# Selecting experts for one half of the tokens beside the gates of the other half

## The chip, the core and the metric

The kernel runs on one NeuronCore of a Trainium2 chip. TensorE multiplies (PE in the profile; its weight loads are PEld), VectorE (DVE), ScalarE (ACT) and GpSimd (POOL) work element by element, and SyncE (SP) issues the DMA transfers. The metric is the device time of one execution in microseconds, and lower is better; times of a kernel are given as the median of the runs shown.

## The reference, cut to what matters

The program is a network of two blocks for 256 tokens with 1024 features, all in fp32. The first block (feed-forward layers, a state-space mixer, neighbourhood attention) and the attention part of the second are not touched. The last stage, `peer`, is:

```python
q = (ht @ w_q).reshape(T, HEADS, 2, half)              # 8 heads, 2 halves of 128 features
s = einsum('thcd,hcnd->thcn', q, sub_keys)             # scores against 128 keys for each half
s1, i1 = top_k(s[:, :, 0], 16)
s2, i2 = top_k(s[:, :, 1], 16)
cand_s = s1[..., :, None] + s2[..., None, :]           # 16 x 16 candidates for a head
top_s, pos = top_k(cand_s, 16)                         # the best 16; pos gives the pair (i1, i2)
gates = softmax(top_s)
experts = i1 * 128 + i2
out = x + sum over (head, k) of gates * gelu(h . u[expert]) * v[expert]
```

## The kernel before

Matmuls are in fp32r with each operand split into a high and a low part, and three products (high by high, high by low, low by high). All weights of the program are one long row of 741 chunks of 128x1024, numbered in the order of use: 469 to 484 are the queries' weights (`peer_q`, one chunk for each of 16 blocks of queries), 485 to 612 the experts' first table (`ut`, two chunks for each of 64 tiles) and 613 to 740 the second table (`v`). The class `Weights` loads a chunk (`w`, 4 buffers), casts its high part on ScalarE (`whi`, line 92) and subtracts the low part (`wlo`), both with 3 buffers. The subtraction is on VectorE (line 96), or on GpSimd (line 94) where the chunk's number modulo 8 is in `ws.on_pool`.

The stage does not gather experts. It computes all of them densely: 64 tiles `c` of the first product (lines 246 to 248), each followed by a GELU into `st` and a store to DRAM (`sd`); then the second product (line 1241), for which each tile is fetched again and multiplied by the gates `gt` (`gate(n)`, line 1221, and a split into high and low parts). The tiles 62 and 63 come first in the second product, since they need no fetch. `gt` has a gate for each of 128 x 128 experts and each of 256 tokens, and fills the large tile `gbig`, in which the scratch of the selection also lies.

The gates come from two generators. `topk_gen(tt)` selects for the 128 tokens of half `tt`: 12 pairs of calls of `top16`, each with ten steps on VectorE (MAX, MAX_INDEX, MATCH_REPLACE), then six 2048-wide steps. `g_gen` takes four tokens at a time: one-hot rows `hot_a` and `hot_g` on VectorE (lines 1131 and 1132), four small matmuls that multiply them (line 1140), and a copy into `gt` on ScalarE (line 1143).

The order is that of the program as the scheduler of the recording layer places it on each engine; within an engine instructions run in that order. The class `Sched` decides what is written between the matmuls: generators in `sc.bg` run one after another, each step yields its cost, and each `tick(budget)` lets so much cost through. Before, `topk_gen(0)`, `topk_gen(1)` and `g_gen()` are appended behind the last query.

`qevac(c)` (line 1163) scales the queries of block `c` from PSUM on VectorE, and `scores(c)` (line 1041 on TensorE, line 1044 on ScalarE) multiplies them by the keys. `by_token` (line 1155) transposes `h`, which `hr` holds after a trip through DRAM. `norm.split` makes the low parts of the first product's input (line 352).

Of the kernel before, what the change touches and what calls it, by code (L numbers as in the profile page):

```python
# [22 lines left out]
T = 256  # L23
# [146 lines left out]
def tile_kernel(ctx: ExitStack, tc: tile.TileContext, A: dict, start: int = 0, end: int = 10):  # L170
# [6 lines left out]
    small = ctx.enter_context(tc.tile_pool(name="small", bufs=3))  # L177
# [840 lines left out]
    def peer(norm):  # L1018
        with tc.tile_pool(name="peer", bufs=2) as p:
            gbig = p.tile([128, 32768], F32, name="gbig", bufs=1)  # L1020
            gt = gbig.rearrange("p (i t) -> p i t", t=T)
            off = [0]

            def carve(n, dt=F32):
                a = gbig[:, off[0]:off[0] + n]
                off[0] += n
# [4 lines left out]
            hr = carve(8 * T).rearrange("p (c t) -> p c t", t=T)  # L1031
            nc.sync.dma_start(hr, hd)
            nc.sync.dma_start(keys, A["keysT"])
            scr = [carve(16 * 128).rearrange("p (c n) -> p c n", n=128) for _ in range(2)]
            i1T, i2T, gaT = (carve(T) for _ in range(3))
# [10 lines left out]
            def top16(rows):  # L1046

                for v, ix, src, tmp in rows:
                    V.max(v[:, 0:8], src)
                for v, ix, src, tmp in rows:  # L1050
                    V.max_index(ix[:, 0:8], v[:, 0:8], src)  # L1051
                for v, ix, src, tmp in rows:
                    V.match_replace(tmp, v[:, 0:8], src, -3.0e38)  # L1053
                for v, ix, src, tmp in rows:
                    V.max(v[:, 8:16], tmp)
                for v, ix, src, tmp in rows:
                    V.max_index(ix[:, 8:16], v[:, 8:16], tmp)  # L1057

            def topk_gen(tt):
                val = carve(256).rearrange("p (c k) -> p c k", k=16)  # L1060
# [17 lines left out]
                yield 1.5  # L1078
                for c in range(0, 8, 2):
                    top16([(tv[:, c + i], pos[:, c + i], cand[:, c + i], tmp[i]) for i in range(2)])  # L1080
                    yield 2.2
# [3 lines left out]
                V.tensor_tensor(e, tv, tv[:, :, 0:1].to_broadcast([128, 8, 16]), op=ALU.subtract)  # L1085
# [15 lines left out]
                yield 1.5  # L1101
# [3 lines left out]
                for c, rank in ((0, af), (1, bf)):  # L1105
                    r = carve(128)
                    V.tensor_tensor(oh.rearrange("p (k a) -> p k a", a=16), rank[:, :, None].to_broadcast([128, 128, 16]),
                                    iota[:, None, 0:16].to_broadcast([128, 128, 16]), op=ALU.is_equal)
                    yield 2.2
                    o4 = oh.rearrange("p (h k a) -> p h k a", h=8, a=16)  # L1110
                    V.tensor_tensor(o4, o4, ix2[:, :, c][:, :, None, :].to_broadcast([128, 8, 16, 16]), op=ALU.mult)
                    yield 2.2
                    V.tensor_reduce(r, oh.rearrange("p (k a) -> p k a", a=16), AX.X, ALU.add)
                    yield 2.2
                    res.append(r)
# [3 lines left out]
                for n, dst in enumerate((i1T, i2T, gaT)):  # L1119
                    S.copy(dst[:, tt * 128:(tt + 1) * 128], pt[:, n * 128:(n + 1) * 128])  # L1120
                yield 0.2

            def g_gen():


                def hots(t0):
                    a = p.tile([128, 4, 128], F32, name="hot_a")
                    g = p.tile([128, 4, 128], F32, name="hot_g")
                    for i in range(4):
                        t = slice(t0 + i, t0 + i + 1)  # L1130
                        V.tensor_scalar(a[:, i], iota, i1T[:, t], None, op0=ALU.is_equal)  # L1131
                        V.tensor_scalar(g[:, i], iota, i2T[:, t], gaT[:, t], op0=ALU.is_equal, op1=ALU.mult)
                    return a, g
                nxt_ = hots(0)
                yield 1.3
                for t0 in range(0, T, 4):
# [4 lines left out]
                    if t0 + 4 < T:  # L1141
                        nxt_ = hots(t0 + 4)
                    S.copy(gt[:, :, t0:t0 + 4].rearrange("p i t -> p t i"), ps.rearrange("p (t i) -> p t i", t=4))
                    yield 1.5


            ht = carve(2 * D).rearrange("p (a d) -> p a d", a=2)
            htd = dram.tile([128, 2, D], F32, name="htd")

            def by_token():  # L1150
                for n in range(4):
                    tt, f = divmod(n, 2)
                    pt = aux()
                    for i in range(4):
                        PE.transpose(pt[:, i * 128:(i + 1) * 128], hr[:, f * 4 + i, tt * 128:(tt + 1) * 128], ident)
# [33 lines left out]
            sgs = {}  # L1189
            for c in range(64):  # L1190
                if c == topk_end:
                    ws.on_pool = ()
                ps = mmtile()
                for i in range(2):
# [4 lines left out]
                    sc.tick(2.35 if c < topk_end else 1.12)  # L1199
# [10 lines left out]
            cx = {}  # L1210
# [7 lines left out]
            def gate(n):  # L1218
                c = V_ORDER[n]
                sg = sgs.pop(c)  # L1220
                tc.keep_in_program_order(V.tensor_mul(sg, sg, gt[:, 2 * c:2 * c + 2, :]))
                i = (n % 4) * 2
                ch, cl = (x[:, i:i + 2] for x in norm.x[:2])
                split2(ch, cl, sg)
                cx[n] = (ch, cl)

            gate(0)
# [225 lines left out]
```

## Time and profile before

| | |
|---|---|
| median of 3 runs | 2394.49 us (2390.14 to 2395.95) |
| the profiled execution | 2397.36 us, span 2395.4 us |
| TensorE busy | 2330.9 us (97%) |
| VectorE busy | 1807.1 us (75%) |
| ScalarE busy | 1327.1 us (55%) |
| GpSimd busy | 373.0 us (16%) |
| mean granted clock of TensorE | 0.99 |

The span goes from the first to the last instruction of the profiled execution; the rest of its time lies around it. A busy share is a mean over all stages, and TensorE's matmuls overlap, so that a gap in TensorE's work is read from the idle time ahead of an instruction, not from the share. The granted clock is 1.00 at 2.4 GHz and 0.5 at 1.2 GHz.

### The profile page before, as it was taken

What the parts mean: (1) busy time and instruction counts of PE and PEld (TensorE: products, weight loads), DVE (VectorE), ACT (ScalarE), POOL (GpSimd) and SP (SyncE); (2) the same over time, 40 slices, a digit from 0 to 9 for tenths busy, and PEclk for the clock granted to TensorE, in tenths of its full rate; (3) what the DMA queues carried; (4) which work ended last, traced back from release to release, by engine and by line L of the source; (5) the groups of instructions that cost most, each with busy time, mean ns of one, the idle gap of its engine ahead of it and who ended that gap; (6) DMA issues with size and microseconds to landing.
All of it is one profiled execution on the core that took longest, in us unless ns stands there. A gap on an engine that the chain in (4) does not pass through costs nothing.

```text
span 2395.4 us, 41145 instructions
## 1 busy us (share of the span) xinstructions
PE 2330.9 (97%) x15646; PEld 2127.0 (89%) x15646; DVE 1807.1 (75%) x3550; ACT 1327.1 (55%) x2081; POOL 373.0 (16%) x309
## 2 busy tenths in 40 slices
PE   8998799999999999999999999998999999999999
PEld 7887798988888889888889999998999999888887
DVE  6777788878768877777768766799777776666666
ACT  6555677746546554566545445554455565444443
POOL 1004788850010000030001000113300000000000
PEclk9999899999999999999999999999999999999999
DMA  6664565546565656435565445655655555777775
GB/s 212 191 191 139 175 197 194 190 142 195 189 190 171 188 186 194 158 125 177 187 189 179 150 137 182 223 177 189 203 183 188 186 189 188 250 242 242 242 241 187
DMA packets 138629, 452.51 MB, mean 189 GB/s; under 512 B 15552, under 2 KB 19648, under 8 KB 137920
## 3 DMA queue, kind: packets, MB, share of 16 engines
q1 hardware_dynamic: 138432, 449.89, 59.1%
q8 instruction: 123, 2.02, 0.3%
q14 instruction: 74, 0.61, 0.1%
HBM read 430.33 MB, written 19.50 MB: 188 GB/s over the span
## 4 chain that ended last, share of the span: by engine, by line
PE 69%; DVE 7%; issue 2%; ACT 1%; DMA 0%; POOL 0%; DVEq 0%; ACTq 0%; POOLq 0%; SPq 0%
PE mm L254 15%; PE aux L1241 15%; PE mm L247 9%; PE mm L248 9%; PE mm L246 9%; PE mm L255 8%; PE aux L1140 2%; DVE wlo L96 2%; DVE x L352 1%; ACT whi L92 1%; PE aux L733 0%; DVE gbig L1051 0%; PE aux L800 0%; DVE gbig L1053 0%; DVE gbig L1057 0%
## 5 line engine op out<-in xcount | busy, mean ns | idle before, releaser
L92 ACT CAST whi<-w 128x1024 fp32r<-128x1024 f32 x740 | 775.5, 1049 | 872.9 <-issue 328.5
L96 DVE TENSOR_TENSOR wlo<-w,whi 128x1024 fp32r<-128x1024 f32 x678 | 845.9, 1248 | 361.8 <-ACT whi L92 359.1
L248 PE MATMUL mm<-x,wlo 128*128 128x256 f32 x2472 | 706.1, 286 | 26.7 <-DVE wlo L96 22.0
L246 PE MATMUL mm<-x,whi 128*128 128x256 f32 x2472 | 718.7, 291 | 3.0 <-ACT acc L552 1.1
L247 PE MATMUL mm<-x,whi 128*128 128x256 f32 x2472 | 705.7, 286 | 2.3 <-DVE x L352 2.2
L254 PE MATMUL mm<-x,whi 128*128 128x512 f32 x1408 | 501.6, 400 | 10.0 <-DVE x L352 10.0
L248 PEld LDWEIGHTS mm<-x,wlo 128*128 128x128 f32 x2472 | 479.1, 194 | 28.6 <-DVE wlo L96 23.4
L246 PEld LDWEIGHTS mm<-x,whi 128*128 128x128 f32 x2472 | 479.1, 194 | 14.6 <-issue 8.4
L247 PEld LDWEIGHTS mm<-x,whi 128*128 128x128 f32 x2472 | 479.4, 194 | 4.2 <-DVE x L352 3.5
L255 PE MATMUL mm<-x,wlo 128*128 128x256 f32 x1408 | 398.6, 283 | 2.1 <-DVE wlo L96 2.1
L254 PEld LDWEIGHTS mm<-x,whi 128*128 128x128 f32 x1408 | 267.6, 190 | 73.7 <-DVE x L352 12.0
L1241 PE MATMUL aux<-whi,x 128*128 128x512 f32 x1024 | 274.1, 390 | 2.0 <-ACT x L362 2.0
L255 PEld LDWEIGHTS mm<-x,wlo 128*128 128x128 f32 x1408 | 270.0, 192 | 3.0 <-DVE wlo L96 2.9
L299 POOL TENSOR_TENSOR sqa<-sqa,sq 128x256 f32<-128x256 f32 x99 | 94.1, 951 | 1141.7 <-ACT sq L298 1135.3
L254 PE MATMUL mm<-a,whi 128*128 128x512 f32 x704 | 246.6, 395 | 0.0
L1241 PEld LDWEIGHTS aux<-whi,x 128*128 128x128 f32 x1024 | 192.2, 188 | 42.0 <-ACT x L362 2.2
L255 PE MATMUL mm<-a,wlo 128*128 128x256 f32 x704 | 197.6, 281 | 0.0
L94 POOL TENSOR_TENSOR wlo<-w,whi 128x1024 fp32r<-128x1024 f32 x62 | 166.7, 2690 | 159.3 <-ACT whi L92 151.1
L254 PEld LDWEIGHTS mm<-a,whi 128*128 128x128 f32 x704 | 132.1, 188 | 30.8
L1241 PE MATMUL aux<-wlo,x 128*128 128x512 f32 x512 | 157.8, 389 | 0.0
L255 PEld LDWEIGHTS mm<-a,wlo 128*128 128x128 f32 x704 | 133.4, 189 | 0.0
L1131 DVE TENSOR_SCALAR hot_a<-cst,gbig 128x128 f32<-128x128 f32 x256 | 72.0, 281 | 63.7 <-PE aux L1140 63.7
(265 smaller groups left out, 2801.2 us busy)
## 6 DMA issues: line engine op xcount, KB each, us to landing
w<-in_gu SPq DMA_DIRECT2D x175, 512.0 KB, 4.1
w<-in_ut SPq DMA_DIRECT2D x128, 512.0 KB, 3.7
w<-in_v SPq DMA_DIRECT2D x128, 512.0 KB, 4.2
w<-in_dn SPq DMA_DIRECT2D x88, 512.0 KB, 4.1
w<-in_ssd_in SPq DMA_DIRECT2D x65, 512.0 KB, 3.8
w<-in_win SPq DMA_DIRECT2D x52, 512.0 KB, 3.6
sd<-st SPq DMA_DIRECT2D x62, 256.0 KB, 2.3
st<-sd SPq DMA_DIRECT2D x62, 256.0 KB, 4.3
```

Source lines behind the costliest of these rows:

```text
L92: nc.scalar.copy(hi, w)
L94: nc.gpsimd.tensor_tensor(lo, w, hi.bitcast(F32), op=ALU.subtract)
L96: nc.vector.tensor_sub(lo, w, hi.bitcast(F32))
L246: PE.matmul(out, wh, xh[:, k], start=start, stop=False, skip_group_check=True)
L247: PE.matmul(out, wh, xl[:, k], start=False, stop=False, skip_group_check=True)
L248: PE.matmul(out, wl, xh[:, k], start=False, stop=stop, skip_group_check=True)
L254: PE.matmul(out, wh, x[:, k], start=start, stop=False, skip_group_check=True)
L255: PE.matmul(out[:, :T], wl, x[:, k, 0], start=False, stop=stop, skip_group_check=True)
L299: G.tensor_tensor(self.acc, self.acc, sq, op=ALU.add)
L1131: V.tensor_scalar(a[:, i], iota, i1T[:, t], None, op0=ALU.is_equal)
L1140: PE.matmul(ps[:, i * 128:(i + 1) * 128], a[:, i], g[:, i], start=True, stop=True)
L1241: PE.matmul(accs[tt * 2 + f], a[:, i, t], b[:, f * 512:(f + 1) * 512], start=n == 0 and i == 0 and b is vh and a is ch, stop=n == 63 and i ...
```

## The change

The tokens are treated in halves. `gbig` is cut in two (`a=2`), the scratch of half 0 lies in the first part and that of half 1 in the second, so that gates of half 0 can be written while half 1 is still selected. `background()` runs the selection of half 0, then the selection of half 1 and the gates of half 0 `together` (in the proportion of their costs), then the gates of half 1. It is appended at query block 6, not behind block 15; scores come two at a time from block 4 on. `hot_a` of four tokens is one 128x512 comparison. `pin` (`tc.keep_in_program_order`) holds the first instruction of most steps in the order of the program, and the costs and budgets are new. GpSimd subtracts for 3 of 8 chunks from query block 6 to tile 13, and for 2 of 8 from tile 14 to the end. The first tile of the second product is gated ahead of the last tile of the first, into `first_h` and `first_l`. `small`, the pool of the norms' small tiles, has 2 buffers.

```diff
-    small = ctx.enter_context(tc.tile_pool(name="small", bufs=3))
+    small = ctx.enter_context(tc.tile_pool(name="small", bufs=2))
...
-            gt = gbig.rearrange("p (i t) -> p i t", t=T)
-            off = [0]
+            gt = gbig.rearrange("p (a i t) -> p a i t", a=2, t=128)
+            off = [0, 16384]
...
+            slots = [[carve(128, half=tt) for _ in range(3)] for tt in range(2)]
...
+            pin = tc.keep_in_program_order
...
-                for v, ix, src, tmp in rows:
-                    V.max(v[:, 0:8], src)
+                for n, (v, ix, src, tmp) in enumerate(rows):
+                    ins = V.max(v[:, 0:8], src)
+                    if n == 0:
+                        pin(ins)
...
-                    yield 2.1
-                V.tensor_copy(ixf, ix)
+                    yield 3.2
+                pin(V.tensor_copy(ixf, ix))
...
-            def g_gen():
+            def g_gen(tt):
+                i1T, i2T, gaT = slots[tt]
...
+                    pin(V.tensor_tensor(a, iota[:, None, :].to_broadcast([128, 4, 128]),
+                                        i1T[:, t0:t0 + 4][:, :, None].to_broadcast([128, 4, 128]), op=ALU.is_equal))
                     for i in range(4):
                         t = slice(t0 + i, t0 + i + 1)
-                        V.tensor_scalar(a[:, i], iota, i1T[:, t], None, op0=ALU.is_equal)
                         V.tensor_scalar(g[:, i], iota, i2T[:, t], gaT[:, t], op0=ALU.is_equal, op1=ALU.mult)
...
+            def together(a, b):
+                run = [[0.0, *a], [0.0, *b]]
+                while run:
+                    e = min(run, key=lambda r: r[0])
+                    try:
+                        c = next(e[1])
+                    except StopIteration:
+                        run.remove(e)
+                        continue
+                    e[0] += c / e[2]
+                    yield c
+
+            def background():
+                yield from topk_gen(0)
+                yield from together((topk_gen(1), 59.0), (g_gen(0), 67.0))
+                yield from g_gen(1)
...
-            norm.ready(lambda: sc.pipe(by_token(), "P"))
+            norm.ready(lambda: sc.later(2, lambda: sc.pipe(by_token(), "P")))
...
-                sc.tick()
+                sc.tick(1.2)
                 norm.ready(lambda c=c, ps=ps: qevac(c, ps))
-                if c == 9:
+                if c == 10:
...
-                if c >= 6 and c % 2 == 0:
-                    scores(done[0])
-                    done[0] += 1
+                if c >= 4 and c % 2 == 0:
+                    for _ in range(2):
+                        scores(done[0])
+                        done[0] += 1
+                if c == 6:
+                    ws.on_pool = (1, 4, 6)
+                    sc.bg.append(background())
...
-            ws.on_pool = (1, 2, 4, 6)
-            sc.bg.append(topk_gen(0))
-            sc.bg.append(topk_gen(1))
-            sc.bg.append(g_gen())
-            topk_end = 18
...
+            def gate(n):
...
+                for tt in range(2):
+                    t = slice(tt * 128, (tt + 1) * 128)
+                    ins = V.tensor_mul(sg[:, :, t], sg[:, :, t], gt[:, tt, 2 * c:2 * c + 2])
...
+                if n == 0:
+                    ch, cl = (p.tile([128, 2, T], F32R, name=f"first_{s}", bufs=1) for s in "hl")
...
             for c in range(64):
-                if c == topk_end:
-                    ws.on_pool = ()
+                if c == 14:
+                    ws.on_pool = (2, 6)
+                if c == 63 and not sc.bg:
+                    gate(0)
...
-                    sc.tick(2.35 if c < topk_end else 1.12)
+                    sc.tick(1.85 if c < 15 else 2.1)
```

The order of VectorE around the end of the queries, first before and then after. Lines 1163 and 1198 are the evacuations of query blocks 14 and 15, line 96 the subtraction of a weight chunk, line 352 the low parts of the first product's input, and MAX, MAX_INDEX and MATCH_REPLACE are steps of the selection.

```order
L1163 TENSOR_TENSOR gbig<-mm,rb 128x256
L96 TENSOR_TENSOR wlo<-w,whi 128x1024
L352 SCALAR_TENSOR_TENSOR x<-gbig,vec,x 128x256 x4
L1163 TENSOR_TENSOR gbig<-mm,rb 128x256
L352 SCALAR_TENSOR_TENSOR x<-gbig,vec,x 128x256 x4
```

```order
L1198 TENSOR_TENSOR gbig<-mm,rb 128x256
L1052 MAX gbig<-gbig 128x8
L1056 MAX_INDEX gbig<-gbig 128x8
L1058 MATCH_REPLACE gbig<-gbig 128x128
L1052 MAX gbig<-gbig 128x8
L1060 MAX gbig<-gbig 128x8
L1052 MAX gbig<-gbig 128x8
L1062 MAX_INDEX gbig<-gbig 128x8
L1056 MAX_INDEX gbig<-gbig 128x8
L352 SCALAR_TENSOR_TENSOR x<-gbig,vec,x 128x256 x5
L1198 TENSOR_TENSOR gbig<-mm,rb 128x256
```

Eight selection steps now stand between the two evacuations, and a subtraction has gone from there (chunk 484 is GpSimd's).

The order of VectorE in the selection, first before (from half 0 to half 1) and then after (half 1 beside the gates of half 0). Lines 1107 and 1111 are 2048-wide steps of the selection, hot_a and hot_g the one-hot rows of the gates.

```order
L96 TENSOR_TENSOR wlo<-w,whi 128x1024
L1111 TENSOR_TENSOR gbig<-gbig 128x2048
L1055 MAX gbig<-gbig 128x8
L1113 TENSOR_REDUCE gbig<-gbig 128x128
L96 TENSOR_TENSOR wlo<-w,whi 128x1024
L1055 MAX gbig<-gbig 128x8
L1057 MAX_INDEX gbig<-gbig 128x8 x2
L1049 MAX gbig<-gbig 128x8 x2
L1051 MAX_INDEX gbig<-gbig 128x8 x2
```

```order
L96 TENSOR_TENSOR wlo<-w,whi 128x1024
L1142 TENSOR_TENSOR hot_a<-cst,gbig 128x512
L1146 TENSOR_SCALAR hot_g<-cst,gbig 128x128 x4
L96 TENSOR_TENSOR wlo<-w,whi 128x1024
L1052 MAX gbig<-gbig 128x8
L1146 TENSOR_SCALAR hot_g<-cst,gbig 128x128
L1056 MAX_INDEX gbig<-gbig 128x8
L1058 MATCH_REPLACE gbig<-gbig 128x128
```

Before, only selection stands between two subtractions; after, one row of the selection alternates with the one-hots of four tokens.

The end of GpSimd's order, as a difference. Line 94 is the subtraction of a weight chunk; the rows above it belong to earlier stages.

```order
 L444 TENSOR_TENSOR pp<-pp,rb 128x256 x8
 L299 TENSOR_TENSOR sqa<-sqa,sq 128x256 x28
-L94 TENSOR_TENSOR wlo<-w,whi 128x1024 x18
-L1449 UNCONDITIONAL_BRANCH
-L1449 ISA
+L94 TENSOR_TENSOR wlo<-w,whi 128x1024 x70
+L1493 UNCONDITIONAL_BRANCH
+L1493 ISA
```

GpSimd's 18 subtractions of this stage become 70, of which 32 fall in the second product.

## Rows read from the trace of the kernel before

**Rows 1.** Busy time by stretch: stretch; us; PE, PEld, DVE, ACT, POOL (instructions); PEclk; DMA; GB/s.
```profile
1620.00:1700.00 80.00, 69.49 (x541) 68.48 (x541) 79.88 (x245) 34.91 (x43) 33.19 (x12) 0.94 0.58 185
1706.00:2040.00 334.00, 332.95 (x2814) 332.96 (x2815) 230.16 (x600) 191.65 (x211) 4.81 (x2) 1.00 0.60 191
2043.00:2391.00 348.00, 348.00 (x1536) 288.03 (x1534) 230.92 (x255) 164.47 (x188) 0.00 (x0) 1.00 0.74 234
```

**Rows 2.** Waits from 1598 to 1710: who for whom, us in total, times, longest.
```profile
PE mm L248 <- DVE wlo L96: 11.6, 5, 6.2
...
PE mm L246 <- ACT whi L92: 0.3, 1, 0.3
```

**Rows 3.** Timeline between the products: start us, us, instruction, [idle before <-releaser].
```profile
2042.62 0.73 PE L1241 MATMUL aux<-whi,x 128*128 128x512 f32 x2 [2.02 <-ACT x L362]
...
2041.96 0.61 ACT L362 CAST x<-st 128x512 fp32r<-128x512 f32 x1
```

**Rows 4.** Timeline of DVE and PE at the end of the queries.
```profile
1590.07 1.23 DVE L96 TENSOR_TENSOR wlo<-w,whi 128x1024 fp32r<-128x1024 f32 x1 [0.53 <-ACT whi L92]
1591.21 1.67 DVE L352 SCALAR_TENSOR_TENSOR x<-gbig,vec,x 128x256 fp32r<-128x256 f32 x4
1592.80 0.42 DVE L1163 TENSOR_TENSOR gbig<-mm,rb 128x256 f32<-128x256 f32 x1
...
1592.23 4.20 PE L1041 MATMUL aux<-gbig 128*128 128x128 f32 x36
```

**Rows 5.** Timeline of DVE, the first steps of two pairs of the selection.
```profile
1598.19 0.47 DVE L1049 MAX8 gbig<-gbig 128x8 f32<-128x128 f32 x2
...
1600.53 0.47 DVE L1049 MAX8 gbig<-gbig 128x8 f32<-128x128 f32 x2
```

**Rows 6.** Groups by line and shape on DVE, 1540 to 2042: count | busy us, mean ns | idle.
```profile
L1107 DVE TENSOR_TENSOR gbig<-gbig,cst 128x2048 f32<-128x2048 f32 x4 | 9.1, 2276 | 0.0
...
L1221 DVE TENSOR_TENSOR st<-st,gbig 128x512 f32<-128x512 f32 x1 | 0.7, 683 | 0.0
```

**Rows 7.** Timeline of DVE at the gates, the one-hots of two tokens.
```profile
1763.08 0.28 DVE L1131 TENSOR_SCALAR hot_a<-cst,gbig 128x128 f32<-128x128 f32 x1
...
1763.53 0.28 DVE L1131 TENSOR_SCALAR hot_a<-cst,gbig 128x128 f32<-128x128 f32 x1
```

**Rows 8.** Timeline of PE around four tokens' gates.
```profile
1725.38 1.06 PE L1140 MATMUL aux<-hot_g,hot_a 128*128 128x128 f32 x8
1726.19 0.36 PE L246 MATMUL mm<-x,whi 128*128 128x256 f32 x1
1726.40 0.28 PE L247 MATMUL mm<-x,whi 128*128 128x256 f32 x1
```

**Rows 9.** Timeline of POOL and DVE during the selection, 1618 to 1707.
```profile
1618.76 2.40 POOL L94 TENSOR_TENSOR wlo<-w,whi 128x1024 fp32r<-128x1024 f32 x1 [2.79 <-ACT whi L92]
...
1618.86 3.38 DVE L96 TENSOR_TENSOR wlo<-w,whi 128x1024 fp32r<-128x1024 f32 x1
...
1629.38 2.55 POOL L94 TENSOR_TENSOR wlo<-w,whi 128x1024 fp32r<-128x1024 f32 x1 [8.23 <-ACT whi L92]
1632.66 4.21 POOL L94 TENSOR_TENSOR wlo<-w,whi 128x1024 fp32r<-128x1024 f32 x1 [0.73 <-ACT whi L92]
...
1629.67 0.27 DVE L1053 MATCH_REPLACE8 gbig<-gbig 128x128 f32<-128x128 f32 x1
...
1632.40 2.28 DVE L1107 TENSOR_TENSOR gbig<-gbig,cst 128x2048 f32<-128x2048 f32 x1
...
1704.62 2.37 DVE L96 TENSOR_TENSOR wlo<-w,whi 128x1024 fp32r<-128x1024 f32 x1
```

**Rows 10.** The page's costliest groups, the cast of a weight chunk.
```profile
L92 ACT CAST whi<-w 128x1024 fp32r<-128x1024 f32 x740 | 775.5, 1049 | 872.9 <-issue 328.5
```

**Rows 11.** Timeline of PE at the first transposes of `h`.
```profile
1550.71 0.63 PE L1155 MATMUL aux<-cst,gbig 128*128 128x128 f32 x4 [1.63 <-DMA gbig<-hd]
```

More of the change, by code (lines that the diff above doesn't have):

```diff
@@ L1106, in topk_gen @@
                     r = carve(128)
-                    V.tensor_tensor(oh.rearrange("p (k a) -> p k a", a=16), rank[:, :, None].to_broadcast([128, 128, 16]),
-                                    iota[:, None, 0:16].to_broadcast([128, 128, 16]), op=ALU.is_equal)
-                    yield 2.2
+                    pin(V.tensor_tensor(oh.rearrange("p (k a) -> p k a", a=16),
+                                        rank[:, :, None].to_broadcast([128, 128, 16]),
+                                        iota[:, None, 0:16].to_broadcast([128, 128, 16]), op=ALU.is_equal))
+                    yield 2.3
                     o4 = oh.rearrange("p (h k a) -> p h k a", h=8, a=16)
[L1111 to L1114, printed above, removed]
+                    pin(V.tensor_tensor(o4, o4, ix2[:, :, c][:, :, None, :].to_broadcast([128, 8, 16, 16]),
+                                        op=ALU.mult))
+                    yield 2.5
+                    pin(V.tensor_reduce(r, oh.rearrange("p (k a) -> p k a", a=16), AX.X, ALU.add))
+                    yield 2.3
                     res.append(r)
@@ L1118, in topk_gen @@
                     PE.transpose(pt[:, n * 128:(n + 1) * 128], src, ident)
-                for n, dst in enumerate((i1T, i2T, gaT)):
-                    S.copy(dst[:, tt * 128:(tt + 1) * 128], pt[:, n * 128:(n + 1) * 128])
+                for n, dst in enumerate(slots[tt]):
+                    S.copy(dst, pt[:, n * 128:(n + 1) * 128])
                 yield 0.2
-            def g_gen():
+            def g_gen(tt):
+                i1T, i2T, gaT = slots[tt]
                 def hots(t0):
@@ L1134, in g_gen @@
                 nxt_ = hots(0)
-                yield 1.3
-                for t0 in range(0, T, 4):
+                yield 2.1
+                for t0 in range(0, 128, 4):
                     a, g = nxt_
@@ L1140, in g_gen @@
                         PE.matmul(ps[:, i * 128:(i + 1) * 128], a[:, i], g[:, i], start=True, stop=True)
-                    if t0 + 4 < T:
+                    if t0 + 4 < 128:
                         nxt_ = hots(t0 + 4)
-                    S.copy(gt[:, :, t0:t0 + 4].rearrange("p i t -> p t i"), ps.rearrange("p (t i) -> p t i", t=4))
-                    yield 1.5
-            ht = carve(2 * D).rearrange("p (a d) -> p a d", a=2)
+                    S.copy(gt[:, tt, :, t0:t0 + 4].rearrange("p i t -> p t i"), ps.rearrange("p (t i) -> p t i", t=4))
+                    yield 2.1
+            def together(a, b):
[13 more added lines that the diff above has]
+                yield from g_gen(1)
+            ht = carve(2 * D, half=1).rearrange("p (a d) -> p a d", a=2)
             htd = dram.tile([128, 2, D], F32, name="htd")
@@ L1181, in peer @@
                 done[0] += 1
[L1182 to L1189 removed]
+            sgs, cx = {}, {}
+            def gate(n):
+                c = V_ORDER[n]
+                sg = sgs.pop(c)
+                for tt in range(2):
+                    t = slice(tt * 128, (tt + 1) * 128)
+                    ins = V.tensor_mul(sg[:, :, t], sg[:, :, t], gt[:, tt, 2 * c:2 * c + 2])
+                    if tt == 0:
+                        pin(ins)
+                if n == 0:
+                    ch, cl = (p.tile([128, 2, T], F32R, name=f"first_{s}", bufs=1) for s in "hl")
+                else:
+                    i = (n % 4) * 2
+                    ch, cl = (x[:, i:i + 2] for x in norm.x[:2])
+                split2(ch, cl, sg)
+                cx[n] = (ch, cl)
             for c in range(64):
[L1191 to L1192 removed]
+                if c == 14:
+                    ws.on_pool = (2, 6)
+                if c == 63 and not sc.bg:
+                    gate(0)
                 ps = mmtile()
@@ L1216, in fetch @@
                     nc.sync.dma_start(sgs[c], sd[c])
[L1218 to L1227, printed above, removed]
+            if 0 not in cx:
+                gate(0)
             for n in range(64):
```

28 lines of the change are left out of this document (16 added, 12 removed).

## Prediction

> **What bounds the kernel now.** I read the stretch table first, then the waits, then the timelines of the places where TensorE waits. In the experts' part TensorE is the engine that everything waits for: in the second product it is busy 348.00 of 348.00 us, and over the gates, 1706 to 2040, 332.95 of 334 [rows 1]. The exception is the selection: from 1620 to 1700 TensorE works 69.49 of 80 us while VectorE works 79.88, and the mean granted clock is 0.94 [rows 1]. The waits of 1598 to 1710 name one cause: five waits of L248 for VectorE's `wlo`, 11.6 us, the longest 6.2 [rows 2]; with one of 0.3 for `whi` that is 11.9. The clock costs (1 - 0.94) x 80 = 4.8 us, of which about 1 fell on idle time: 4.0. So the selection costs TensorE about 16 us. A second, single wait stands between the products: 2.02 us, until ScalarE's cast at 2041.96 [rows 3].
>
> Why VectorE is late: I count its instructions by weight chunk (469 to 484 queries, 485 to 612 first table, 613 to 740 second table) in the order before, and price them by the time from one start to the next. A `wlo` costs 1.14 (1590.07 to 1591.21) [rows 4], ten selection steps for two rows 2.34 (1598.19 to 1600.53) [rows 5], a 2048-wide step 2.2 [rows 6], one token's two one-hots 0.45 (1763.08 to 1763.53) [rows 7]. Chunks 485 to 519: 19 x 1.14 + 20.1 x 2.34 + 12 x 2.2 + 8 x 0.4 (the `x` low parts [rows 4]) + 8 x 0.45 + some 7 for small steps = 109 us. TensorE needs 24 matmuls of 0.12 a chunk (2814 in 332.95 us [rows 1]), 2.88, and 0.9 for four tokens' gates (1725.38 to 1726.19, and 0.09 more on the matmul behind) [rows 8]: 35 x 2.88 + 0.9 = 102 us. On top, POOL and VectorE stop each other. A `wlo` on VectorE that starts 0.1 us behind POOL's takes 3.38 instead of 1.23 and ends 1.1 behind POOL's end; POOL's at 1632.66 takes 4.21 instead of 2.40 behind a VectorE step that has 2 us to go; a selection step runs through in 0.27 under a POOL piece [rows 4, 9]. Six VectorE instructions are held like this between 1618.86 and 1704.62 (3.38 and 2.37 are the first and the last), about 11.6 us in all [rows 9]. 109 + 11.6 - 102 = 19 us; a `wlo` may be late by the two chunks that its buffers are ahead, less cast (1.05 [rows 10]), subtraction and hand-overs: 5.75 - 1.05 - 1.2 - 0.2 = 3.3. That leaves 15.5 us, against the 16 read. The account closes, so I use it for the change.
>
> **The change, part by part.** *Selection of half 0 begun among the queries, selection of half 1 beside the gates of half 0, `wlo` between the steps.* The order after, with the same prices and 1.65 for four tokens' one-hots: chunks 485 to 510 hold 16 x 1.14 + 9.5 x 2.34 + 5 x 2.2 + 8 x 0.4 + 4 = 59 us of VectorE against 26 x 2.88 = 75 of TensorE. Chunks 511 to 576 hold 50 x 1.14 + 8 x 2.34 + 7 x 2.2 + 35 x 1.65 + 3 = 152 against 66 x 2.88 + 35 x 0.9 = 221. Chunks 577 to 605 hold 73 against 110. None is over TensorE's time, so the 16 us go: -16.0. What hides the selection is TensorE's own work, 75 and 221 us; without that cover it would cost its 109.
>
> *The one-hot `hot_a` as one 128x512 instruction.* Not in the trace. Bounds: 0.57, a quarter of the 2048-wide comparison [rows 6], and 0.68, the 512-wide product L1221 [rows 6]; I take 0.61, as a comparison with the same spread inputs. It replaces four that take 0.8 together. VectorE has idle time there, so either end is worth 0.
>
> *POOL: 70 subtractions instead of 18.* In the selection there are fewer of them (3 or 2 of 8 chunks, not 4), but they go on through gates and second product. Price of one on VectorE: 11.6 / 18 = 0.65 as measured; its upper end is 2.4, a whole POOL piece [rows 9]. In chunks 485 to 510 there are 10: 59 + 6.5 = 65 of 75 by the measured price, 59 + 24 = 83 by the upper end, which is 83 - 75 - 3.3 = 4.7 us of waiting. In 511 to 576 there are 16: 190 of 221 at the upper end. But a `wlo` can be late by itself while the sum is good: in the order after, the steps between two `wlo` leave some 2.8 us before TensorE would wait, and a POOL piece may take 2.4 of them and ScalarE's own queue 1.1. I put 2.0 us on this, between 0 and 4.7, nearer to the lower end because of the measured price.
>
> *POOL in the second product, 32 pieces.* The cast may start two chunks (2 x 2.72) before its use, so POOL has 5.4 us for 1.05 + 2.4 + at most 1.2 behind a `wlo`: 4.7. VectorE has 96 x 1.14 + 128 x 0.34 + 64 x 0.6 = 191 us, with 32 x 2.4 = 77 at most held, in 348. I take 0; the upper end is a rival below.
>
> *Queries.* All scores of before wait in one burst of 44 matmuls of 0.12 (36 of them at 1592.23 in 4.20 us) [rows 4], which covers the last query's evacuation on VectorE. After, two queries' scores follow every second query and only three stand ahead of the last. VectorE does between the evacuations of queries 14 and 15: 0.34 + 8 steps of 0.23 + 5 x 0.4 + 0.42 = 4.6, with a hand-over of some 0.2 at each end 5.0; TensorE has 2.88 + 3 x 0.48 = 4.3 to do. It waits 0.7. POOL's piece of chunk 486 starts a cast (1.05) after query 14 and ends 3.5 after it; the five `x` steps would begin 2.2 after it. If they are held, 1.3 is added: 2.0, or 2.1 with one more hand-over. I take 2.1, because those steps read two tiles as the held `wlo` does; lower end 0.7. Queued behind this evacuation are the scores, then chunk 485 on TensorE and the next casts on ScalarE.
>
> *First gating ahead of the last tile, one `first_h/first_l` more.* Its multiply, cast and subtraction are done in the 5.8 us of chunks 611 and 612, so the 2.02 goes: -2.0 (lower end 1.9). The split of the multiply into two halves adds about 0.15 us per gating, on an engine that is busy 230.92 of 348 us [rows 1]: 0.
>
> *`by_token` two turns later.* Its transposes wait 1.63 us for the copy of `h` [rows 11]; in the order after they stand one matmul, 0.12 us, later. -0.1, left out. *`small` with two buffers:* nothing in the order ahead of the queries moves: 0. *The new credits and the pins* act through the order alone, which is counted above.
>
> **Sum.** 2395.4 - 16.0 - 2.0 + 2.1 + 2.0 = 2381.5 span; with the 2.0 us around it 2383.5, against 2397.4 of the profiled execution, -13.9. That execution lies 2.9 over the median of the runs shown, 2394.5, so I expect a median of 2380.5.
>
> The Trainium skill, "SBUF — State Buffer", section "Who interferes with whom", says that VectorE and GpSimd share one port pair under an exclusive lock, that a VectorE instruction with two SBUF inputs or in a two-port mode takes part, and that the later one waits for the whole of the other. The 3.38 and the 4.21 of rows 9 agree, and so does the selection step that runs through. By it every POOL piece costs the upper end of 2.4, which speaks against the 52 more; the sum would be 2383.2 instead of 2380.5. It is the mechanism of the second case here.
>
> **The rivals.** *B, POOL's pieces hold VectorE where it has no time to give.* For it: the six held instructions, and 26 pieces in chunks 485 to 576, in tight steps. Against it: selection steps are not held, and the sums leave 10 us in the first stretch at the measured price, and 31 in the second even at the upper end. At 4.7 in the first stretch, 2.1 at the queries and 0.3 for each of 16 pieces in the second, 4.8, it gives back 11.6: 2394.5 - 18 + 11.6 = 2388. A wait of the length of the one at 1638 would bring the lower clock again, up to 2393. *C, slower: POOL is late in the second product.* If a piece waits behind VectorE by more than 5.4 - 1.05 - 2.4 = 2.0 us, TensorE waits for `wlo` in a stage that had no wait. One piece did take 4.21 [rows 9], 1.8 more than alone. At 0.7 us for each of 32 it is 22 us: 2402. It decides from 0.5 us a piece on. Against it: the longest VectorE step there is a `wlo`, 1.2, not one of 2.2. *D, the change doesn't do it:* the scores or the transposes of half 0 come so late that the steps bunch up again, the 16 us stay and only the 2.0 goes while the queries add 2.1: 2394.5. Against it: the counts of the order above.
>
> **Chances.** The forecast 0.74 (2375 to 2387, no new wait to 6.5 us more), B 0.14, C 0.06, D 0.06. I take 0.3%, 7.2 us, as what a measurement of this kernel can tell from no change: 2387.3 and below is faster. B lies mostly inside it: 0.04 faster, 0.10 same. Faster 0.78, same 0.16, slower 0.06. The range goes from 2374 to 2390: it takes in both ends of the unknown prices (-18 + 0.7 and -18 + 6.8) and the near half of B, and leaves out C, D and the rest of B.
>
> **What would show it.** Right: VectorE no longer full in any 20 us of the selection, no wait over 2.5 us of L248 for `wlo`, clock 1.00 from the queries to the end, one wait of 1 to 2 us at the last scores, none between the products, TensorE 348.0 in the second product. Wrong: repeated waits for `wlo` next to POOL pieces (B), TensorE under 348 of 348 in the second product, waiting for L94 (C), VectorE full over 50 us or more (D).

## The result and the profile after

The changed kernel takes 2420.39 us (median of 4 runs, 2414.72 to 2425.46) against 2395.22 of the kernel before (median of 4, 2390.14 to 2397.93): ratio 1.0105, 95% interval 1.0083 to 1.0127. It is slower by some 25 us, where 14 us less were forecast. The profiled execution has a span of 2419.5 us.

The time splits into two parts of opposite sign. From the first evacuation of a query block to the first matmul of the second product it was 2042.62 - 1548.0 = 494.6 us before and is 2021.11 - 1546.3 = 474.8 after: -19.8. From there to the end of the last matmul of the second product it was 348.5 and is 393.6: +45.1. The sum is +25.3.

The first part, busy time by stretch of the changed kernel, answers to the first two of [rows 1]:

```profile
1600.00:1620.00 20.00, 20.00 (x169) 20.00 (x169) 16.91 (x67) 10.60 (x12) 7.36 (x3) 1.00 0.73 221
...
1660.00:1680.00 20.00, 19.92 (x167) 19.69 (x167) 17.99 (x26) 9.26 (x13) 6.89 (x2) 1.00 0.76 230
...
1720.00:2020.00 300.00, 300.00 (x2537) 300.00 (x2537) 228.81 (x456) 174.46 (x194) 55.14 (x22) 1.00 0.60 189
2043.00:2391.00 348.00, 322.45 (x1347) 248.34 (x1347) 238.36 (x252) 140.61 (x169) 67.93 (x28) 1.00 0.69 214
```

In the selection VectorE leaves at least 2 us free in each 20, TensorE is full and its clock 1.00. The last row is the same stretch as the third of [rows 1]: TensorE was busy for all 348.00 us and now for 322.45, with 1347 matmuls in place of 1536.

TensorE's waits from 1540 to 2042, which answer to [rows 2, 3, 11]:

```profile
PE aux L1285 <- DVE x L363: 0.8, 1, 0.8
PE aux L1044 <- ACT gbig L1047: 0.7, 1, 0.7
PE mm L247 <- DVE x L352: 0.4, 1, 0.4
PE aux L1285 <- DVE first_l L363: 0.3, 1, 0.3
```

No wait for `wlo` is left of the 11.6 us, and the 2.02 between the products is gone; 0.3 and 0.8 come behind the first matmuls of the second product. The waits of the second product, from 2042 to 2415, are new; before, TensorE had none in this stretch:

```profile
ACT x L362 <- DVE st L1230: 216.0, 59, 6.2
DVE st L1230 <- DMA st<-sd: 66.9, 28, 3.7
PEld aux L1285 <- DVE wlo L96: 48.2, 54, 1.8
PE aux L1285 <- DVE wlo L96: 24.3, 46, 1.4
...
PE aux L1285 <- POOL wlo L94: 0.3, 1, 0.3
```

TensorE waits for the low parts that VectorE makes, almost never for those of GpSimd. VectorE in turn stands still 28 times for the fetch of a tile (`sd` into `st`), ahead of the gate multiply L1230. The timeline of VectorE, GpSimd and SyncE over two tiles shows how the two belong together:

```profile
2100.40 0.43 DVE L1230 TENSOR_TENSOR st<-st,gbig 128x256 f32<-128x256 f32 x1 [2.41 <-DMA st<-sd]
2100.74 1.22 DVE L96 TENSOR_TENSOR wlo<-w,whi 128x1024 fp32r<-128x1024 f32 x1
2101.87 0.42 DVE L1230 TENSOR_TENSOR st<-st,gbig 128x256 f32<-128x256 f32 x1
2102.98 0.69 DVE L363 TENSOR_TENSOR x<-st,x 128x512 fp32r<-128x512 f32 x1 [0.69 <-ACT x L362]
2103.70 0.33 SPq L1268 DMA_DIRECT2D st<-sd  x1
2103.93 1.23 DVE L96 TENSOR_TENSOR wlo<-w,whi 128x1024 fp32r<-128x1024 f32 x1 [0.26 <-ACT whi L92]
2104.98 2.43 POOL L94 TENSOR_TENSOR wlo<-w,whi 128x1024 fp32r<-128x1024 f32 x1 [10.13 <-ACT whi L92]
2105.07 2.95 DVE L1230 TENSOR_TENSOR st<-st,gbig 128x256 f32<-128x256 f32 x2
2108.38 0.69 DVE L363 TENSOR_TENSOR x<-st,x 128x512 fp32r<-128x512 f32 x1 [0.35 <-ACT x L362]
2109.10 0.33 SPq L1268 DMA_DIRECT2D st<-sd  x1
...
2112.91 0.43 DVE L1230 TENSOR_TENSOR st<-st,gbig 128x256 f32<-128x256 f32 x1 [2.36 <-DMA st<-sd]
```

L363 ends at 2103.67 and at 2109.07, and each time a fetch is issued 0.03 us later: it waited for the buffer that L363 gave back. The multiply at 2112.91 waits for the fetch of 2109.10, and L96, for which TensorE waits, is queued behind it. Four chunks take 2112.91 - 2100.40 = 12.51 us here, where TensorE alone needs 10.9. The chain of work that ended last runs through the same instructions (start us, us, what; the stretch from 2090 to 2116):

```profile
2096.53 3.77 DMA st<-sd
...
2100.74 1.22 DVE wlo L96
...
2102.85 1.06 ACT whi L92
...
2103.93 1.23 DVE wlo L96
2105.16 2.54 DVE st L1230
...
2108.38 0.70 DVE x L363
...
2109.10 3.72 DMA st<-sd
```

TensorE isn't in it. One fetch and one multiply that took 2.54 us beside a GpSimd subtraction (called a piece from here on) are the two long links, and so there are two suspects: the order that puts a fetch into the chain, and the holding, by which a multiply that starts just behind a piece takes 2.54 us instead of 0.42.

### The profile page after: what moved, and what is told of

Read it like the earlier page. It is cut to its first block, busy times and chain, and to the rows that moved or that the text cites. A ratio compares the mean times of both kernels' runs of the same rounds, so it can differ in the third digit from the quotient of the medians.

```text
span 2419.5 us, 41219 instructions
## 1 busy us (share of the span) xinstructions
PE 2343.0 (97%) x15646; PEld 2114.9 (87%) x15646; DVE 1840.4 (76%) x3370; ACT 1318.8 (55%) x2081; POOL 499.0 (21%) x361
## 3 DMA queue, kind: packets, MB, share of 16 engines
q8 instruction: 123, 2.02, 0.3%
## 4 chain that ended last, share of the span: by engine, by line
PE 57%; DVE 11%; DMA 5%; ACT 3%; issue 3%; POOL 0%; ACTq 0%; DVEq 0%; SPq 0%; POOLq 0%
PE mm L254 15%; PE mm L247 9%; PE mm L246 9%; PE mm L248 9%; PE mm L255 8%; DMA st<-sd 5%; DVE wlo L96 4%; DVE st L1230 3%; PE aux L1154 2%; ACT whi L92 2%; PE aux L1285 2%; DVE x L352 1%; DVE x L363 1%; ACT x L362 1%; PE aux L733 0%
## 5 line engine op out<-in xcount | busy, mean ns | idle before, releaser
L96 DVE TENSOR_TENSOR wlo<-w,whi 128x1024 fp32r<-128x1024 f32 x626 | 779.0, 1245 | 256.7 <-ACT whi L92 253.7
L248 PE MATMUL mm<-x,wlo 128*128 128x256 f32 x2472 | 702.5, 284 | 15.6 <-DVE wlo L96 10.6
L94 POOL TENSOR_TENSOR wlo<-w,whi 128x1024 fp32r<-128x1024 f32 x114 | 292.8, 2569 | 718.7 <-ACT whi L92 685.8
L1285 PE MATMUL aux<-wlo,x 128*128 128x512 f32 x504 | 162.2, 403 | 25.7 <-DVE wlo L96 24.3
L1230 DVE TENSOR_TENSOR st<-st,gbig 128x256 f32<-128x256 f32 x128 | 115.3, 919 | 74.9 <-DMA st<-sd 74.7
L362 ACT CAST x<-st 128x512 fp32r<-128x512 f32 x63 | 39.1, 621 | 216.9 <-DVE st L1230 216.9
```

The lines of the kernel that those rows point to most:

```text
L94: nc.gpsimd.tensor_tensor(lo, w, hi.bitcast(F32), op=ALU.subtract)
L96: nc.vector.tensor_sub(lo, w, hi.bitcast(F32))
L248: PE.matmul(out, wl, xh[:, k], start=False, stop=stop, skip_group_check=True)
L362: S.copy(hi, src)
L1230: ins = V.tensor_mul(sg[:, :, t], sg[:, :, t], gt[:, tt, 2 * c:2 * c + 2])
L1285: PE.matmul(accs[tt * 2 + f], a[:, i, t], b[:, f * 512:(f + 1) * 512], start=n == 0 and i == 0 and b is vh and a is ch, stop=n == 63 and i ...
```

## Theories

**O, the order.** The gate multiply became two halves, and only the first is pinned. The pin holds it behind what stands ahead of it in the program, no pin holds the second half, and VectorE's order at the end of the second product became (words in brackets are what an instruction waits for):

```
L1230 TENSOR_TENSOR st<-st,gbig 128x2x128
L1230 TENSOR_TENSOR st<-st,gbig 128x2x128 [waits DMAHW3_49,DVE_49]
L363 TENSOR_TENSOR x<-st,x 128x2x256 [waits Activation_49]
L96 TENSOR_TENSOR wlo<-w,whi 128x1024 [waits DMAHW1_49,Activation_49]
L96 TENSOR_TENSOR wlo<-w,whi 128x1024 [waits DMAHW2_49,Activation_49]
L1230 TENSOR_TENSOR st<-st,gbig 128x2x128
L363 TENSOR_TENSOR x<-st,x 128x2x256 [waits Activation_49]
L96 TENSOR_TENSOR wlo<-w,whi 128x1024 [waits DMAHW4_49,Activation_49]
L1230 TENSOR_TENSOR st<-st,gbig 128x2x128
L363 TENSOR_TENSOR x<-st,x 128x2x256 [waits Activation_49]
```

Number the tiles by their turn, 0 to 63. The waiting multiply is the first half of tile 63; three L363 (tiles 61, 62, 63) and two second halves (62, 63) still follow. So the first half of tile m+2 stands ahead of L363 of tile m, while before it was multiply m, L363 m, multiply m+1 throughout. With three buffers of `st` the fetch of tile m+2 can't start before L363 of tile m-1 has ended. The fetch, 3.7 us, must therefore land between two neighbouring L363, and if it hasn't, VectorE's queue stands. From the issue of a fetch to the multiply that uses it there are 3.8 us now (2109.10 to 2112.91); in the trace of before there were 12.9, tile after tile.

**H, the holding.** GpSimd's 32 pieces of the second product hold the second half 2.2 us each (2.62 in place of 0.42); everything else follows from that. This is the second rival's place, with another wait in it. **B:** three buffers of `st` are too few for a fetch of 3.7 us.

## The experiments

The second product is given from its first matmul to the end of its last, read from the traces; ratios are to runs of the kernel before on the same chip. In e3 and e4 one piece stays (chunk 614, subtracted ahead of the edit), and in e6 and e7 that chunk is VectorE's.

| kernel | gate multiply | pieces on GpSimd | second product, us | median, us | ratio, 95% |
|---|---|---|---|---|---|
| before | one, pinned | 0 | 348.5 | 2395.2 | |
| after | halves, first pinned | 32 | 393.6 | 2420.4 | 1.0083 to 1.0127 |
| e1 | one, pinned | 32 | 348.9 | 2377.7 | 0.9893 to 0.9944 |
| e2 | halves, both pinned | 32 | 348.9 | 2379.2 | 0.9908 to 0.9956 |
| e3 | halves, first pinned | 1 | 362.6 | 2388.2 | 0.9949 to 0.9990 |
| e4 | one, pinned | 1 | 348.9 | 2380.9 | 0.9910 to 0.9960 |
| e5, of before | halves, first pinned | 0 | 357.3 | 2405.1 | 1.0024 to 1.0055 |
| e6, of before | halves, first pinned | 31 | 394.6 | 2438.8 | 1.0156 to 1.0202 |
| e7, of before | one, pinned | 31 | 350.1 | 2396.9 | 0.9988 to 1.0019 |
| e8, four `st` | halves, first pinned | 32 | 392.4 | 2418.7 | 1.0071 to 1.0119 |
| e9, pieces of 512 | halves, first pinned | 64 | 402.8 | 2428.8 | 1.0107 to 1.0168 |
| e10, later start | one, pinned | 32 | 348.9 | 2377.3 | 0.9901 to 0.9948 |
| e11, no GpSimd | one, pinned | 0 | 348.3 | 2369.3 | 0.9860 to 0.9918 |
| e12, gated later | one, pinned | 32 | 349.0 | 2373.6 | 0.9888 to 0.9947 |

**e1, one multiply.**

```diff
-                for tt in range(2):
-                    t = slice(tt * 128, (tt + 1) * 128)
-                    ins = V.tensor_mul(sg[:, :, t], sg[:, :, t], gt[:, tt, 2 * c:2 * c + 2])
-                    if tt == 0:
-                        pin(ins)
+                sv = sg.rearrange("p i (a t) -> p a i t", a=2)
+                pin(V.tensor_mul(sv, sv, gt[:, :, 2 * c:2 * c + 2]))
```

> The changed kernel with one 128x512 gate multiply for each tile, pinned, in place of two of 128x256 of which only the first is pinned; GpSimd keeps its 32 subtractions in the second product. Theory O (order): with only the first half pinned, the first half of tile m+2 stands ahead of the low part (L363) of tile m on VectorE, and its fetch can only be issued when tile m-1 gives its buffer back, so that one fetch of 3.7 us lies in the chain of every tile. With one multiply the order is again multiply m, L363 m, multiply m+1, and the second product takes 348 us instead of some 393: 2373 to 2379 us in all. Theory H (holding): GpSimd's 32 pieces hold the multiply 2.2 us each, which delays the buffers; they stay, so the kernel stays at 2405 us or more.

2377.67 us, and 348.9 us in the second product: all 45 us are back, with GpSimd's pieces in place. Its timeline of VectorE, GpSimd and SyncE:

```profile
2108.91 0.69 DVE L363 TENSOR_TENSOR x<-st,x 128x512 fp32r<-128x512 f32 x1
2109.51 0.69 DVE L1229 TENSOR_TENSOR st<-st,gbig 128x512 f32<-128x512 f32 x1
2109.62 0.33 SPq L1265 DMA_DIRECT2D st<-sd  x1
2110.59 2.39 POOL L94 TENSOR_TENSOR wlo<-w,whi 128x1024 fp32r<-128x1024 f32 x1 [8.49 <-ACT whi L92]
2111.01 2.53 DVE L363 TENSOR_TENSOR x<-st,x 128x512 fp32r<-128x512 f32 x1 [0.81 <-ACT x L362]
```

The holding is still there: L363 takes 2.53 us instead of 0.69 behind a piece of 2.39. But a multiply follows the issue of its fetch by 10.8 or 14.4 us and doesn't wait for it, and TensorE has no wait from 2030 to the end of the stage. H by itself falls: in this order (multiply m, L363 of tile m, multiply m+1; the good order from here on) the holding costs nothing. The Trainium skill, "SBUF — State Buffer", section "Who interferes with whom", says that the later of two such instructions is blocked for the whole of the other; the 2.53 agrees. What it costs the kernel is another matter.

**e2, both halves pinned.** Only `if tt == 0:` is gone, so that the second half stands directly behind the first.

> The changed kernel with both halves of the gate multiply pinned; still two multiplies of 128x256, still 32 pieces on GpSimd. Theory O: the second half follows the first at once, L363 of tile m stands ahead of the first half of tile m+1, and the time is 2373 to 2380 us: the splitting itself costs nothing, only where the halves stand. Theory H: no change, 2415 to 2422. A third theory, that two multiplies are too much work for VectorE: also no change, 2415 to 2422, where the single multiply recovers.

2379.19 us, second product 348.9. Two multiplies of 0.42 us in place of one of 0.68 cost nothing that can be seen; where they stand was all.

**e3, GpSimd's pieces taken out of the second product; e4, that and one multiply.**

```diff
+            ws.on_pool = ()
             if 0 not in cx:
                 gate(0)
```

> The changed kernel with no GpSimd subtraction in the second product (VectorE does all 128 chunks there); the halved multiply and its one pin as they are. Theory H: the whole loss is gone, 2371 to 2378 us. Theory O: the halves still run ahead of their tile, but two first halves now come together and two L363 after them, so that one fetch (3.7 us) lies in the chain of every two tiles instead of one for each; worked out 3.7 + 0.1 + 0.4 + 3 x 1.15 (wlo) + 2 x 0.42 + 2 x 0.69 + 0.7 = 10.6 us against TensorE's 10.9 for two tiles, so it is about covered: 2373 to 2390. This one alone doesn't tell the theories apart; with the single multiply it does.

> Both edits: one pinned multiply, and no GpSimd subtraction in the second product. Both theories: 2371 to 2378 us, TensorE 348 of 348 us there. It tells what GpSimd's 32 pieces cost where the order is good: theory O says within 2 us of the single multiply with GpSimd; theory H says 30 us or more under it.

e4 has 348.9 us like e1, so the pieces cost nothing in the good order; its 2380.89 us in all lies 3 over the expected range. e3 has 2388.21 us and 362.6 in the second product: taking the pieces away gives back 31 of the 45 us, but how much of that is the holding this run doesn't tell, since VectorE's order differs too. Two first halves now come together, then two L363:

```profile
2106.62 0.69 DVE L363 TENSOR_TENSOR x<-st,x 128x512 fp32r<-128x512 f32 x1 [0.69 <-ACT x L362]
2110.37 0.43 DVE L1230 TENSOR_TENSOR st<-st,gbig 128x256 f32<-128x256 f32 x1 [3.06 <-DMA st<-sd]
...
2112.36 0.42 DVE L1230 TENSOR_TENSOR st<-st,gbig 128x256 f32<-128x256 f32 x1 [0.43 <-DMA st<-sd]
...
DMA to landing us min/median/max: 2.9/5.2/7.3
```

The last line is the tile `st` from 2060 to 2360. I had priced the fetch at 3.7 us; here it takes 5.2 in the median (no run shows why), and the 10.6 us for a pair of tiles became 362.6 / 32 = 11.3, over TensorE's 10.9.

**e5 to e7, the suspects put into the kernel before.** e5 writes its multiply in halves, e6 adds `ws.on_pool = (2, 6)` ahead of the second product, e7 has that alone.

```diff
-                tc.keep_in_program_order(V.tensor_mul(sg, sg, gt[:, 2 * c:2 * c + 2, :]))
+                for tt in range(2):
+                    t = slice(tt * 128, (tt + 1) * 128)
+                    ins = V.tensor_mul(sg[:, :, t], sg[:, :, t], gt[:, 2 * c:2 * c + 2, t])
+                    if tt == 0:
+                        tc.keep_in_program_order(ins)
```

> The kernel before with one edit: its gate multiply is written as two halves of the tokens, the first pinned, as in the change. No GpSimd piece in the second product. Theory O: the order of the halves is as in the changed kernel without GpSimd there, so the second product takes the 362.6 us measured there instead of 348: 2395.4 + 14.6 = 2410 us (2403 to 2415). Theory H: no piece, no holding, 2393 to 2399.

> The kernel before with the halved multiply, first half pinned, and with GpSimd subtracting 2 of 8 chunks in the second product: the two suspects alone, nothing of the selection's change. Theory O: one fetch in the chain of every tile, the 393.6 us of the changed kernel instead of 348: 2395.4 + 45.6 = 2441 us (2432 to 2447). If something else of the change were needed for the loss: under 2415.

> The kernel before with GpSimd subtracting 2 of 8 chunks in the second product, and its one multiply as it was. Theory O: the order stays good, 2393 to 2399 us. Theory H: 32 x 0.7 to 1.4 us of waiting, 2417 to 2440.

e7 is the kernel before's equal (2396.89), e5 a little slower (2405.11; 357.3 us in the second product, not the 362.6 taken over from e3), and e6 has the whole loss (2438.84). In the second product: +1.6, +8.8 and +46.1 us. The 1.6 of e7 is TensorE's clock, 0.91 on the mean from 2040 to 2060, behind a wait of 2.0 us between the products; from 2060 on TensorE is full at 1.00:

```profile
2040.00:2060.00 20.00, 19.04 (x77) 15.53 (x78) 12.80 (x13) 8.54 (x11) 2.40 (x1) 0.91 0.67 219
2060.00:2200.00 140.00, 140.00 (x619) 115.99 (x618) 101.91 (x90) 67.60 (x78) 31.11 (x13) 1.00 0.77 248
```

The two edits are harmless or cheap apart and cost 46 together. The pieces do two things to the free halves: they hold them, and they change the order that they fall into, from a first half that stands ahead of L363 by one and by two tiles in turn (e3, e5) to one that stands two ahead throughout (the changed kernel, e6). Nothing of the selection's part is needed. The waits of e6, 2045 to 2430, read like those of the changed kernel:

```profile
DVE st L1223 <- DMA st<-sd: 75.9, 32, 4.6
...
PE aux L1246 <- DVE wlo L96: 25.8, 43, 2.3
```

**e8, four buffers of `st`.** `bufs=4` at both places; `first_h` and `first_l` take the places of `hot_a` and `hot_g`, to make room.

> The changed kernel with four buffers of st instead of three (first_h and first_l take the places of hot_a and hot_g, to make room); multiply, pin and GpSimd as in the change. A rival B: three buffers are too few for a fetch of 3.7 us; a fourth gives a fetch one tile more, and the time falls to 2374 to 2382 us. Theory O: the first half, which nothing but the fetch holds back, moves one tile further ahead in the order (the first half of tile m+3 ahead of L363 of tile m), the fetch stays in the chain: 2412 to 2425 us.

2418.68 us, no change; B falls. The order explains it: four L363 now follow the first half of tile 63, so the first half moved one tile further ahead, and the fetch is as late as before:

```profile
2108.90 0.33 SPq L1268 DMA_DIRECT2D st<-sd  x1
...
2112.67 0.43 DVE L1230 TENSOR_TENSOR st<-st,gbig 128x256 f32<-128x256 f32 x1 [2.31 <-DMA st<-sd]
```

**e9, the piece in two.** VectorE's order is that of the changed kernel, and only the holding was to get shorter. (The subtractions of VectorE are line 99 here, the multiply is 1233.)

```diff
-                nc.gpsimd.tensor_tensor(lo, w, hi.bitcast(F32), op=ALU.subtract)
+                k = 512 if self.ns >= 613 else 1024
+                for j in range(0, 1024, k):
+                    nc.gpsimd.tensor_tensor(lo[:, j:j + k], w[:, j:j + k], hi[:, j:j + k].bitcast(F32),
+                                            op=ALU.subtract)
```

> The changed kernel with each GpSimd subtraction of the second product cut in two of 128x512; VectorE's order is the same, instruction by instruction, so only the holding changes: a held second half waits some 1.2 us less. If the holding is the whole cost of each pair of tiles (theory H): 1.2 x 32 = 38 us come back, 2382 us (2376 to 2388). Theory O: behind the held instruction stands one that waits for a fetch issued at 2103.70 and there 3.7 later, 0.2 before the hold ends, and L362 and L363 can gain at most 0.6 us a pair by it: 0 to 0.6 x 32 = 18 us, 2402 to 2420.

2428.79 us, above both expectations. The holding did get shorter, and nothing came back:

```profile
2101.01 2.77 POOL L96 TENSOR_TENSOR wlo<-w,whi 128x512 fp32r<-128x512 f32 x2 [10.16 <-ACT whi L92]
...
2101.10 1.52 DVE L1233 TENSOR_TENSOR st<-st,gbig 128x256 f32<-128x256 f32 x1
2103.00 1.05 DVE L1233 TENSOR_TENSOR st<-st,gbig 128x256 f32<-128x256 f32 x1 [0.39 <-DMA st<-sd]
```

The second half takes 1.52 instead of some 2.6. Behind it stands a first half that waits for its fetch until 2103.00, and the second piece holds that one too (1.05). In the changed kernel the fetch at this place had landed 3.2 us after 2103.70, at 2106.9, and the multiply in front was held until 2107.7 (the row of 2105.07 in the timeline above joins two multiplies; this is the view of the tile `st` from 2103 to 2108):

```profile
L1230 DVE TENSOR_TENSOR st<-st,gbig x2: 411/1514/2616, 2105.1 to 2107.6; 128x256 f32<-128x256 f32 x2
...
DMA to landing us min/median/max: 3.2/3.2/3.2
```

So in every second tile it was the holding and not the fetch that ended last there. From the start of the held multiply to L363 it took 3.31 us, and in e9 it takes 2.88: only 0.4 us of the holding is gone, not 1.2. The other fetch of each pair of tiles takes 4.4 us in the median now, not 3.7, and that is more than was won; no run shows why. Of the 9.2 us by which the second product got longer, (1 - 0.91) x 20 = 1.8 is TensorE's clock, 0.91 on the mean from 2020 to 2040. VectorE waits for fetches 46 times and 100.8 us between 2050 and 2400, not 28 times and 66.9, and the fetch's share of the chain there is 57%, not 31%. So e9 doesn't settle what the holding costs in this order.

An estimate from the trace of the changed kernel gives a size: without the holding the first half could begin at 2107.0, when its fetch has landed, and L363 at 2107.3 instead of 2108.38, 1.0 us earlier. Over the 28 pairs of tiles of this kind in the trace this adds up to some 27 of the 45 us, if the fetches take as long as they did.

**e10 to e12, steps of the first part, each on top of e1.** e10 appends `background()` behind the last query instead of at query block 6. e11 leaves out both lines that set `ws.on_pool`, `(1, 4, 6)` and `(2, 6)`, so that GpSimd does nothing from the queries on. e12 leaves out the call `gate(0)` ahead of tile 63, and the gating is written behind the last tile, as before.

> The changed kernel with one gate multiply (as in the first experiment), and the background of selection and gates appended behind the last query, as before the change, instead of at query block 6. If the treatment in halves is what spreads VectorE's work: 2375 to 2382 us, TensorE full from 1620 on with waits under 2 us in all. If the early start is needed: VectorE is full over 40 us or more behind the queries and TensorE waits for its wlo by 5 to 12 us: 2382 to 2390.

> The changed kernel with one gate multiply and without any GpSimd subtraction from the queries on (none in selection, gates and second product). By the sums of the prediction VectorE then has 70 of 75 us in chunks 485 to 510 and 170 of 221 in the next 66: no wait, 2374 to 2381 us, so that the pieces that made trouble weren't needed. Rival: the sum hides tight steps, TensorE waits for wlo by 5 us or more in the selection: 2382 to 2392.

> The changed kernel with one gate multiply, and its first gating behind the last tile of the first product, as before the change. The trace has one wait of about 2 us at the first matmul of the second product, where the single multiply with the gating ahead has 0.3 to 1.1: 2376 to 2382 us. If the gating ahead is hidden anyway: no such wait, 2374 to 2380.

e10 is e1's equal (2377.32): VectorE has at most 18.62 of 20 us from 1600 to 1720 and TensorE is full there, so the early start isn't needed. Which of the other steps spreads the work (the halves side by side, the pins, the budgets, the single `hot_a`) no run shows one by one. e11 is the fastest kernel of the study, 2369.26 us, 5 under its expected range and faster than both kernels that were given. VectorE gets nearly full for once, and TensorE doesn't wait:

```profile
1600.00:1620.00 20.00, 20.00 (x169) 20.00 (x169) 19.93 (x86) 10.63 (x12) 0.00 (x0) 1.00 0.70 226
```

From 1535 to 2042 e11 has a single wait of TensorE, 0.4 us for L352. None of the 70 subtractions on GpSimd was needed. Its interval against e1's overlaps a little, so of the 8 us between them I count only what the traces show: 822.1 against 827.4 us from the first evacuation to the end of the second product, of which 2.2 is a wait for the copy of `h`, which comes and goes between executions.

e12 (2373.64 us, just under both expected ranges) has no wait of 2 us: it is 0.3 for `first_l`, as in the changed kernel and e1. Where the call is written makes no difference, since the cast starts 1.85 us ahead of the first matmul of the second product in e1 and in e12. Before, the cast into `x` stood on ScalarE behind the last tile's GELU (2041.96 [rows 3]); with buffers of its own, `first_h` and `first_l`, it stands ahead of it. That these buffers are what removes the 2.02 is argued from this; no run takes them away by themselves.

## Why the prediction was wrong

*The selection, -16.0:* right. TensorE is full, the clock stays at 1.00 and no wait for `wlo` is left. The first part gained 19.8, more than the 14 of the sum, for the most part since the losses set against it didn't come: *GpSimd in selection and gates, +2.0*, was 0, the lower end; *the queries, +2.1*, was 0.7 (0.68 at the last scores), the lower end too, but not as the sum has it: one of the `x` steps took 1.39 us in place of 0.47 behind a piece, and e11, without pieces, has no wait there at all. *The first gating, -2.0*, gave 1.7: 0.3 is left, and the 0.8 at the second tile is missing in e1 and belongs to the order of the second product. *`hot_a`*, priced at 0.61, takes 0.69 in the median, just over its upper end, and is hidden, 0. *`by_token`, -0.1*, left out: its wait was 1.63 before, absent in the changed kernel, and 0 to 2.6 in the others, so that 1.6 of the 19.8 is luck.

**The step that failed is in the second product: "The split of the multiply into two halves adds about 0.15 us per gating, on an engine that is busy 230.92 of 348 us: 0."** The 0.15 was right (2 x 0.42 against 0.69), and e2 shows that it costs nothing. But I priced the busy time of an instruction and didn't ask where its two parts stand. "The new credits and the pins act through the order alone, which is counted above" was not so: I counted the order of the queries, the selection and the gates, not that of the second product. There a free half let the next tiles' first halves run ahead, and a wait for a fetch, which VectorE had never had in this stage, came to stand in front of the `wlo`.

*GpSimd in the second product, 0, with rival C (2402) as the upper end:* with one multiply the step was right, e1 and e7 show 0. Rival C had the place, and its 22 us were half of what came, but its mechanism was wrong: TensorE waits 24.3 us for VectorE's `wlo` and 0.3 for GpSimd's. The pieces are one half of the cause, through the order and the holding: without them the halves cost 13.7 (e3) or 8.8 (e5), with them 45 to 46. The 77 us of holding were set against VectorE's idle time of the whole stage; once a fetch and L363 hang on the held half, the idle time elsewhere doesn't pay for it. What I took for independent, an edit at 0 and another at 0, was not.

How the loss divides between order and holding stays open: every kernel that took the pieces away had another order too, and e9, which kept the order, shortened the holding by 0.4 us only and moved the fetches with it. That the order is needed for the loss is shown (e1, e2), and that the holding costs nothing in the good order. In the changed order the multiply that the pieces hold lies in the chain (L1230 makes 22% of it from 2050 to 2400), and the estimate under e9 gives it some 27 of the 45 us; the rest, 18, is near the 13.7 that the halves cost without pieces in e3.

## What to carry to other kernels

An edit on an idle engine is free only if its instructions stand in the same places: where one pinned instruction is split, pin all its parts, and read the order at every stage that the edit touches, not only at the one that it is meant for. Look for the loop of a buffer's release, the transfer that waits for it and the instruction that waits for the transfer, and count how many turns of the work lie between them; another buffer didn't help here, because the waiting instruction moved ahead with it. Edits that cost 0 and 9 us apart cost 46 together, so run each new helper with and without the others.

## What the runs showed of the hardware

A VectorE multiply of 0.42 us takes 2.6 when it starts 0.1 behind a GpSimd subtraction of 2.43, and an L363 2.53 instead of 0.69; cut in two pieces of 1.3 to 1.5, GpSimd's work holds two VectorE instructions in turn, 1.52 and 1.05, and takes 2.77 in all. The same 256 KB fetch lands 3.5, 4.3 or 5.2 us after its issue in the median, in the changed kernel, the one before and e3. A price read in one order did not hold in another.
